# A two-layer hybrid trunk on one core: TensorE in the order of the source, with the mixers' steps placed by a running estimate of each engine's time

## The chip, the cores and the metric

The kernel runs on one core of a Trainium2 chip. The metric is the device time of one execution in microseconds (us), taken as the median of several runs. The profile of one execution gives the time of every instruction on TensorE (PE), VectorE (DVE), ScalarE (ACT), GpSimd (POOL) and of the DMA issues on SyncE (SP).

## The reference

One inference step of a decoder trunk with two layers, for a prompt of 256 tokens and 8 x 4 sample tokens with the same weights, so 288 columns. All is float32, and the width is 1024.

```python
def mixer_block(x, ...):                      # x += mixer_block(x)
    h = rmsnorm(x, p['norm_mix_g'])
    (q_a, k_a, v_a, x_b, y_b, q_c, k_c, v_c, r_c, a_c, g_a, g_b, g_c) = jnp.split(h @ p['w_in'], offs, axis=-1)
    ...   # o_a: sliding-window attention (swa), 8 heads, 2 K/V heads, window 128, sinks
    xc, new_lru_buf = causal_dwconv(x_b, lru_buf, p['lru_conv_w'], p['lru_conv_b'])
    hr, new_h = rg_lru(xc, lru_h, ...)        # gates, then h[t] = a[t] h[t-1] + b[t]   (the scan)
    o_b = jax.nn.gelu(y_b) * hr
    log_alpha = jax.nn.log_sigmoid((a_c @ p['gla_wa2'] + p['gla_ba']).astype(F32)) / GLA_TAU
    o, new_s = gla(q_c * GLA_DK ** -0.5, k_c, v_c, log_alpha, gla_s)     # chunks of 32 tokens
    o_c = rmsnorm(o, p['gla_on_g']) * jax.nn.silu(r_c)
    merged = (jax.nn.sigmoid(g_a) * (o_a @ p['w_branch_a']) + jax.nn.sigmoid(g_b) * (o_b @ p['w_branch_b'])
              + jax.nn.sigmoid(g_c) * (o_c @ p['w_branch_c']))
    return merged @ p['w_out'], ...

x = x + mix
x = x + cross_attn(rmsnorm(x, p['norm_x_g']), mk, mv, p)   # 4 heads over 256 memory tokens
x = x + conv_ffn(rmsnorm(x, p['norm_ffn_g']), ffn_buf, p)  # up, causal conv of 3, SwiGLU, down
```

## The kernel before, in words

**Projections.** A product with a weight matrix goes tile by tile. `weights` (from L149) loads a 128 x 1024 tile by a DMA on SyncE into `wst` (4 buffers, L157), ScalarE rounds it to fp32r (`whi`, 3 buffers, L158), VectorE forms the rest (`wlo`, 3 buffers, L159). `mm3` (L177 to L179) then issues three fp32r matmuls for each 128 rows of the contraction: whi with the high part of the activations, whi with their low part, wlo with the high part. A weight load waits until L159 has read the buffer that it overwrites. The products of two tiles go to one pair in PSUM (`mm`, 2 buffers); small products go to the PSUM pool `sm` (4 buffers).

**Order of a layer.** `mixers` computes Q, K, V of the attention, the low-rank gate input `ac` of gla (L1361, 8 matmuls), then the projections for gla (`qk`, `vf`), lru (`xb`, `gy`), the output gate `sr`, and then gate(0), gate(1), branch(0), branch(1), gate(2), branch(2), with branch 0, 1, 2 for swa, lru, gla; then `wout`, added to the residual X. `cross` and `ffn` follow. Each norm's gain goes into the activations, and its factor `rbc` is multiplied in at the eviction of the products.

**Chains.** The mixers' own small fp32 work is written as generators: `swa` (L462), `lru` (L684), `gla` (L751), norms, memory norms and more. Each step between two `yield`s issues some matmuls and the work of other engines around them. `proj` calls `tick` after every 4 of its 8 contraction blocks (12 matmuls); `tick` (L167) adds to each active chain the credit that the table RATE gives for the current place and runs a step for each whole unit. `Chain.finish` runs what is left.

**Who sets the order.** The text gives an order of instructions; the tile framework then places them on each engine by its own reckoning of readiness and priority (`tc.high_priority`). Only the opening (first norm, Q, K, V of layer 0) is under `manual_schedule`, where the listed engines keep the order of the source. So a step's matmuls can be split up, interleaved with weight matmuls, or moved.

**Lines that the prediction speaks of.** swa: L557 scores (64-row halves), L582 normalizing of the probabilities on VectorE, L586 their transposes, L596 the product with V, L608 the load of its value cache `swav`, L621, L648, L657, L668 the sample part. gla: L755 load of `wa2` (128 KB), L760 its product with `ac`, L816, L846 and L848 scores of a chunk and their masking, L853, L866, L883, L893, L923, L932 states and outputs. lru: L686 `wax`, L688 `lh`, L709 gates, L734 the scan. L242, L219, L253 are the norms, L1092 the load of memory keys, L978 that of the memory itself, L1000 and L1011 its norm.

Of the kernel before, what the change touches and what calls it, by code (L numbers as in the profile page):

```python
# [46 lines left out]
RATE = [  # L47
    dict(swa=1, gla=1),
    dict(swa=4.5, gla=0.5),
    dict(swa=4.5, gla=3.5),  # L50
    dict(swa=5, gla=1),
    dict(swa=4, gla=5),
    dict(swa=5, gla=0.5, lru=3),
    dict(swa=4, gla=4.5, lru=2.5),
    dict(swa=0.5, gla=3, lru=6),
    dict(gla=2.5, lru=2),
    dict(gla=1.5, lru=4),
    dict(gla=5),
    dict(gla=4),
]  # L60

WAIT = 4

PACE = dict(late=(1, 0), mem=(2.5, -2), norm=(3, -1), keys=(2, -0.5), factors=(3.5, -1), flips=(1.5, 1))


# [16 lines left out]
def trunk(ctx: ExitStack, tc: tile.TileContext, a: dict):  # L83
# [7 lines left out]
    gp = ctx.enter_context(tc.tile_pool(name="gp", bufs=8))  # L91
# [70 lines left out]
    pace = dict(rates={}, chains={}, credit={})  # L162

    def pacing(rates, chains, credit):
        pace.update(rates=rates, chains=chains, credit={c: credit for c in rates})

    def tick():  # L167

        for c, n in pace["rates"].items():
            if c in pace["chains"]:  # L170
                pace["credit"][c] = pace["credit"].get(c, 0.0) + n / 4
                while pace["credit"][c] >= 1:
                    pace["credit"][c] -= 1
                    pace["chains"][c].step(1)
# [47 lines left out]
    def norm_prep(l, col):  # L222

        for k in range(KD):
# [4 lines left out]
        for k in range(0, KD, 2):  # L229
# [3 lines left out]
            sqs.append(sq[:, :T])  # L233
        yield
        return (yield from norm_factors(sqs))

    def norm_factors(sqs):
# [12 lines left out]
        yield from wait(2)  # L250
# [42 lines left out]
    def wait(n):  # L293
        for _ in range(n):
            yield

# [28 lines left out]
    class Chain:  # L325
        def __init__(self, gen):
            self.gen, self.out, self.done = gen, None, False

        def step(self, n):
            for _ in range(n):  # L330
                if self.done:
                    return
                try:
                    next(self.gen)
                except StopIteration as e:
                    self.out, self.done = e.value, True

        def finish(self):
            while not self.done:
                self.step(1)  # L340
            return self.out

    def norm_chain(l, col):

        norm = Chain(norm_prep(l, col))
        norm.step(1)
        pacing(dict(n=PACE["norm"][0]), dict(n=norm), PACE["norm"][1])
        return norm

    def opening():  # L350
# [70 lines left out]
        norm = Chain(norm_factors(sqs))  # L421
        pacing(dict(n=4), dict(n=norm), -1)

        def rest(i, out):
            for k in range(KD):
                c = slice(k * P, (k + 1) * P)
                mm3(out[:, :T], hi[i][:, c], lo[i][:, c], xh[:, k, :], xl[:, k, :], k == 0, k == KD - 1)
                if k % 4 == 3:
                    tick()
# [32 lines left out]
    def swa(l, Q, KV):  # L462
# [140 lines left out]


# [79 lines left out]
    def lru(l, xb, gy):  # L684
# [66 lines left out]
    def gla(l, got):  # L751
# [191 lines left out]


# [9 lines left out]
        yield from wait(WAIT)  # L954
# [18 lines left out]
    def mem_load(l, mh, ml):  # L973
# [5 lines left out]
        yield  # L979
# [126 lines left out]
    def cross(l, mem, mh, ml, kcs, vcs):  # L1106
        norm = norm_chain(l, C_GX)
        pace["rates"]["m"], pace["chains"]["m"] = PACE["late"][0], mem
        pace["credit"]["m"] = PACE["late"][1]
        km = mem_k(l, mem, mh, ml)  # L1110
        rbc = norm.finish()
        knorm = Chain(mem_k_norm(l, km))
        knorm.step(1)
        pacing(dict(n=PACE["keys"][0]), dict(n=knorm), PACE["keys"][1])
        Q, sq, qp = s5t(), s5t(), s5t()
        G.memset(qp, 0.0)
        for h in (0, 2):
# [3 lines left out]
            hs = slice(h, h + 2)  # L1121
            with tc.high_priority(AHEAD):
# [27 lines left out]
        pacing(dict(n=PACE["factors"][0]), dict(n=fac), PACE["factors"][1])  # L1150
# [71 lines left out]
        pacing(dict(n=PACE["flips"][0]), dict(n=flip_s), PACE["flips"][1])  # L1222
# [39 lines left out]
    def ffn(l):  # L1262
# [7 lines left out]
        def up(c):  # L1270
            pm = pmm()
# [377 lines left out]
```

## Time and profile before

| what | us |
|---|---|
| median of 3 runs | 1139.26 (1138.72 to 1141.09) |
| the profiled execution, its own time | 1139.73 |
| its span | 1137.8 |
| TensorE busy | 1121.8 (99%) |
| VectorE busy | 794.6 (70%) |
| ScalarE busy | 617.5 (54%) |
| GpSimd busy | 254.3 (22%) |

The span runs from the first to the last instruction; the execution's own time is 1.9 us longer. Matmuls are pipelined, so that a matmul's length (about 0.30 us for 288 columns) is longer than the distance of two starts; distances of starts tell what TensorE spends. An fp32 matmul has two records. Names of buffers are shown without their numbers: `s` is an activation tile of SBUF, `g` a wide one, `m` a narrow one, `sm` and `mm` PSUM.

### The profile page before, as it was taken

The page shows a single profiled execution, that of the slowest core. Times are in us where ns is not written, and L with a number is a line of the kernel's source. Part 1 is how long each engine was busy: PE and PEld are TensorE (multiplying, and loading weights), DVE is VectorE, ACT ScalarE, POOL GpSimd, SP SyncE. Part 2 cuts the span into 40 slices and gives each one's busy share as a digit, 9 for nine tenths or more (in the row PEclk, how much of TensorE's full clock was granted, in tenths as well). Part 3 has the DMA queues.
Part 4 walks back from the last instruction along what each step waited for, and adds up shares of the span by engine and source line. Part 5 has one row for each costly group of instructions (what it writes and reads, how often), then busy time and mean ns, then how long its engine had stood idle before and what let it go on. Part 6 is the DMA issues. An engine that isn't in the chain of part 4 may idle for free.

```text
span 1137.8 us, 22342 instructions
## 1 busy us (share of the span) xinstructions
PE 1121.8 (99%) x8846; PEld 1063.3 (93%) x8846; DVE 794.6 (70%) x1451; ACT 617.5 (54%) x961; POOL 254.3 (22%) x426
## 2 busy tenths in 40 slices
PE   9999999999999999999999999999999999999998
PEld 8878799999989999999999887999999899999998
DVE  6776586757775887885457775856686678888743
ACT  6545874345555665654445567643464456566532
POOL 0211020201211455550012200202111024555400
PEclk9999999999999999999999999999999999999999
DMA  8844445558466455556545343455585644554662
GB/s 284 274 132 129 131 154 167 157 172 316 154 224 232 149 159 162 163 152 206 173 160 176 119 130 117 139 186 167 187 303 153 202 143 149 167 165 154 185 192 83
DMA packets 62663, 198.11 MB, mean 174 GB/s; under 512 B 7960, under 2 KB 11768, under 8 KB 62560
## 3 DMA queue, kind: packets, MB, share of 16 engines
q1 hardware_dynamic: 59536, 188.55, 51.9%
q0 software_dynamic: 2880, 8.15, 2.0%
q8 instruction: 69, 1.13, 0.4%
q14 instruction: 34, 0.28, 0.1%
q10 hardware_dynamic: 144, 0.00, 0.0%
HBM read 187.35 MB, written 8.95 MB: 173 GB/s over the span
## 4 chain that ended last, share of the span: by engine, by line
PE 90%; DVE 4%; ACT 3%; DMA 2%; issue 1%; POOL 0%; SPq 0%; ACTq 0%; POOLq 0%; DVEq 0%
PE mm L178 25%; PE mm L179 25%; PE mm L177 25%; DVE wlo L159 2%; PE sm L596 1%; ACT whi L158 1%; DMA wst<-in_win 1%; PE sm L557 1%; PE sm L1047 1%; PE sm L932 1%; PE sm L1048 1%; PE sm L1049 1%; PE sm L586 1%; PE sm L1234 1%; PE mm L1173 1%
## 5 line engine op out<-in xcount | busy, mean ns | idle before, releaser
L159 DVE TENSOR_TENSOR wlo<-wst,whi 128x1024 fp32r<-128x1024 f32 (+1 forms) x302 | 374.1, 1240 | 141.8 <-ACT whi L158 140.5
L158 ACT CAST whi<-wst 128x1024 fp32r<-128x1024 f32 (+1 forms) x302 | 312.4, 1036 | 273.0 <-PE mm L178 217.2
L177 PE MATMUL mm<-xh,whi 128*128 128x288 f32 x1536 | 455.7, 297 | 1.4 <-DVE s L1329 1.4
L179 PE MATMUL mm<-xh,wlo 128*128 128x288 f32 x1536 | 456.5, 297 | 0.0
L178 PE MATMUL mm<-xl,whi 128*128 128x288 f32 x1536 | 456.1, 297 | 0.0
L177 PEld LDWEIGHTS mm<-xh,whi 128*128 128x128 f32 x1536 | 289.3, 188 | 8.7 <-issue 5.0
L179 PEld LDWEIGHTS mm<-xh,wlo 128*128 128x128 f32 x1536 | 289.0, 188 | 4.3 <-issue 2.9
L178 PEld LDWEIGHTS mm<-xl,whi 128*128 128x128 f32 x1536 | 289.1, 188 | 3.7 <-DVE xl L227 2.1
L178 PE MATMUL mm<-s,whi 128*128 128x288 f32 (+1 forms) x756 | 222.9, 295 | 1.9 <-DVE s L192 1.9
L177 PE MATMUL mm<-s,whi 128*128 128x288 f32 (+1 forms) x756 | 223.5, 296 | 0.0
L179 PE MATMUL mm<-s,wlo 128*128 128x288 f32 (+1 forms) x756 | 222.1, 294 | 0.0
L178 PEld LDWEIGHTS mm<-s,whi 128*128 128x128 f32 x756 | 142.1, 188 | 2.9 <-DVE s L192 2.8
L177 PEld LDWEIGHTS mm<-s,whi 128*128 128x128 f32 x756 | 142.0, 188 | 2.0 <-issue 1.3
L179 PEld LDWEIGHTS mm<-s,wlo 128*128 128x128 f32 x756 | 142.2, 188 | 0.6 <-DVE wlo L159 0.3
L1296 DVE SCALAR_TENSOR_TENSOR y<-u,prm,y 128x304 f32<-128x304 f32 x176 | 82.5, 524 | 0.0
L1300 POOL TENSOR_TENSOR m<-y 128x256 f32<-128x256 f32 x44 | 60.7, 1380 | 69.1 <-ACT y L1297 66.2
L191 ACT CAST s<-m 128x288 fp32r<-128x288 f32 (+1 forms) x46 | 19.6, 426 | 72.2 <-POOL m L1301 72.2
L1294 ACT ACTIVATE y<-u,prm 128x304 f32<-128x304 f32 x88 | 51.8, 635 | 11.7 <-DVE u L1287 11.7
L1436 POOL TENSOR_TENSOR g<-g,g 128x576 f32<-128x576 f32 x12 | 21.0, 1749 | 160.5 <-DVE g L1434 160.5
L192 DVE TENSOR_TENSOR s<-m,s 128x288 fp32r<-128x288 f32 (+1 forms) x46 | 20.8, 452 | 50.8 <-ACT s L191 50.8
L1283 POOL COPY u<-s 128x32 f32<-128x32 f32 x44 | 46.3, 1053 | 0.6 <-DMA s<-in_fconv 0.6
L232 POOL TENSOR_TENSOR s<-s 128x288 f32<-128x288 f32 x20 | 19.2, 966 | 119.3 <-ACT s L231 119.3
(386 smaller groups left out, 1221.7 us busy)
## 6 DMA issues: line engine op xcount, KB each, us to landing
wst<-in_win SPq DMA_DIRECT2D x98, 512.0 KB, 3.5
wst<-in_up SPq DMA_DIRECT2D x88, 512.0 KB, 3.5
wst<-in_down SPq DMA_DIRECT2D x32, 512.0 KB, 3.7
wst<-in_wbr SPq DMA_DIRECT2D x24, 512.0 KB, 3.5
s<-in_mk SPq DMA_DIRECT2D x16, 512.0 KB, 6.6
wst<-in_wout SPq DMA_DIRECT2D x16, 512.0 KB, 4.2
wst<-in_down SPq DMA_DIRECT2D x16, 384.0 KB, 3.1
g<-in_mv SPq DMA_DIRECT2D x16, 256.0 KB, 4.3
```

The lines of the kernel that those rows point to most:

```text
L158: A.copy(hi[:, :n], st[:, :n])
L159: (E or V).tensor_sub(lo[:, :n], st[:, :n], hi[:, :n].bitcast(F32))
L177: PE.matmul(out, wh, bh, start=first, stop=False)
L178: PE.matmul(out, wh, bl, start=False, stop=False)
L179: PE.matmul(out, wl, bh, start=False, stop=last)
L191: A.copy(hi, src)
L192: V.tensor_sub(lo, src, hi.bitcast(F32))
L1283: G.tensor_copy(us[:, :, :, 0:2], fhist[:, 2 * c : 2 * c + 2])
L1294: A.activation(y[:, i, :WFO], u[:, i, 2:], AF.Identity, scale=w[2], bias=prm[:, l, C_FCB + f : C_FCB + f + 1])
L1296: V.scalar_tensor_tensor(y[:, i, :WFO], u[:, i, j : j + WFO], w[j], y[:, i, :WFO], ALU.mult, ALU.add)
L1300: G.tensor_mul(h[:, :NP_], y[:, 0, :NP_], y[:, 1, :NP_])
L1436: (G if x == 1 or m < KD - 4 else V).tensor_add(acc[m], acc[m], g)
```

## The change

All work of the two layers now runs under `manual_schedule` for TensorE: its instructions keep the order of the source. The other engines are scheduled as before. The tables RATE, WAIT and PACE are gone. Instead a callback, `account`, sees each instruction as it is issued and keeps a running time: `est["pe"]` for TensorE, one for each other engine, and `est["cur"]` for the step being issued. DMA copies are skipped. A chain's next step may run at the first `tick` at which `est["pe"]` has reached the end of its last step's estimated work plus 0.3 us. `tick` is called after every 2 contraction blocks (6 matmuls). `lru` yields until `gla` has finished. The memory chain starts ahead of gate(2) rather than behind branch(2). In layer 1, K and V go to two `sm` tiles before the norm is finished; in `ffn` a third pair of up does; in `cross` the norm is finished after the first pair of wq. The `g` pool has 11 buffers instead of 8.

```diff
-    gp = ctx.enter_context(tc.tile_pool(name="gp", bufs=8))
+    gp = ctx.enter_context(tc.tile_pool(name="gp", bufs=11))
...
+    est = dict(pe=0.0, cur=None, serial=True, busy={})
+    active = {}
+
+    def account(i):
+
+        if not hasattr(i, "engine") or not i.outs or i.opcode == "DMACopy":
+            return
+        e, n = str(i.engine), 1
+        for _, c in i.outs[0].ap[1:]:
+            n *= c
+        if i.opcode == "Matmult":
...
+            est["pe"] = max(est["pe"], est["cur"] or 0.0) + c
+            if est["cur"] is not None:
+                est["cur"] = est["pe"]
+            return
+        c = {"EngineType.DVE": 0.1 + n / 850, "EngineType.Activation": 0.22 + n / 1200}.get(e, 0.15 + n / 600)
+        cur = est["cur"] if est["cur"] is not None and est["serial"] else est["pe"]
+        t = est["busy"][e] = max(est["busy"].get(e, 0.0), cur) + c
+        if est["cur"] is not None:
+            est["cur"] = max(est["cur"], t + 0.1)
+
+    nc.push_inst_callback(account)
 
     def tick():
 
-        for c, n in pace["rates"].items():
...
+        for c in list(active.values()):
+            while not c.done and c.ready <= est["pe"]:
+                c.step()
+
+    class Chain:
...
+        def step(self):
+            est["cur"] = est["pe"]
+            try:
+                more = next(self.gen)
+            except StopIteration as e:
+                self.out, self.done, more = e.value, True, 0.0
+            self.ready = est["cur"] + 0.3 + (more or 0.0)
+            est["cur"] = None
+
+        def finish(self):
+            while not self.done:
+                c = min((c for c in [self, *active.values()] if not c.done), key=lambda c: c.ready)
+                est["pe"] = max(est["pe"], c.ready)
+                c.step()
+            return self.out
...
-            if k % 4 == 3:
+            if k % 2:
                 tick()
...
-    def lru(l, xb, gy):
+    def lru(l, got, xb, gy):
+        while "gla" not in got:
+            yield
...
-        yield from wait(WAIT)
...
-        rbc = norm.finish()
-        knorm = Chain(mem_k_norm(l, km))
...
+            rbc = norm.finish()
             with tc.high_priority(AHEAD):
                 V.tensor_mul(Q[:, hs], pm[:, :, :T], bc(rbc, 2))
...
-        first = [up(0), up(1)]
+        first = [up(0), up(1), up(2, (None, psm(), psm()))]
         rbc = norm.finish()
...
             first = [win(I_Q, 2), win(I_Q + 2, 2)]
+            kv = [psm(), psm()]
+            for j in range(2):
+                proj(kv[j][:, :T], a["win"][l, I_K + j], KD, lambda k: xh[:, k, :], lambda k: xl[:, k, :])
             rbc = norm.finish()
...
-        gate(0, 7)
-        gate(1, 8)
-        branch(0, 9)
-        branch(1, 10)
-        gate(2, 11)
-        branch(2, 11)
+        gate(0)
+        gate(1)
+        branch(0)
+        branch(1)
         mh = [s5v(4, NP_, F32R), s5v(4, NP_, F32R)]
         ml = [s5v(4, NP_, F32R), s5v(4, NP_, F32R)]
-        mem = Chain(mem_load(l, mh, ml))
-        mem.step(1)
-        pacing(dict(n=PACE["mem"][0]), dict(n=mem), PACE["mem"][1])
+        mem = active["mem"] = Chain(mem_load(l, mh, ml))
+        gate(2)
+        branch(2)
...
-    for l in range(L):
-        cross(l, *mixers(l))
-        ffn(l)
+    with tc.manual_schedule(engines={mybir.EngineType.PE}):
+        for l in range(L):
+            cross(l, *mixers(l))
+            ffn(l)
+    nc.remove_inst_callback(account)
...
-    nc = bacc.Bacc("TRN2", target_bir_lowering=False, num_devices=1)
+    nc = bacc.Bacc("TRN2", target_bir_lowering=False, num_devices=1, dynamic_dma_scratch_size=8192)
```

The following pieces show the order on an engine; the lines of the changed kernel have numbers of their own (L204 to L206 are L177 to L179 of before, L474 and L475 are L466 and L467, L771 is L760, L857 is L846, L859 is L848, L590 is L582). `sm_461<-m_413,m_457` reads: written to sm, from m 413 and m 457.

TensorE, layer 0, around the first step of gla (m_503 before and m_457 after are wa2, m_411 and m_413 are ac). Before, 74 weight matmuls after L1361:

```order
L179 MATMUL mm_514<-xh,wlo_517 128x288
L177 MATMUL mm_514<-xh,whi_587 128x288
L178 MATMUL mm_514<-xl,whi_587 128x288
L760 MATMUL sm_507<-m_411,m_503 128x288
L760 MATMUL sm_510<-m_411,m_503 128x288
L493 MATMUL sm_533<-s_495,cst 32x256 x4
L494 MATMUL sm_534<-m_496,cst 32x288
```

After, six weight matmuls after the same 8 matmuls:

```order
L204 MATMUL mm_416<-xh,whi_418 128x288
L205 MATMUL mm_416<-xl,whi_418 128x288
L206 MATMUL mm_416<-xh,wlo_419 128x288
L474 MATMUL sm_429<-cst,s_91 128x128 x2
L475 MATMUL sm_429<-cst,s_91 32x128
L771 MATMUL sm_461<-m_413,m_457 128x288
L771 MATMUL sm_464<-m_413,m_457 128x288
```

The product with wa2 has moved ahead by 68 weight matmuls.

SyncE, layer 0, the loads around wa2 (in_wa). Before:

```order
L686 DMA s_1193<-in_wax 128x1024
L157 DMA wst_745<-in_win 128x1024
L688 DMA lh_1195<-in_lh 128x32
L608 DMA s_1248<-in_swav 128x1024
L157 DMA wst_793<-in_win 128x1024
L755 DMA m_503<-in_wa 128x256
L1092 DMA s_2957<-in_mk 128x1024
```

After:

```order
L697 DMA s_1717<-in_wax 128x1024
L137 DMA wst_706<-in_win 128x1024
L699 DMA lh_1719<-in_lh 128x32
L617 DMA s_1813<-in_swav 128x1024
L1103 DMA s_3008<-in_mk 128x1024
L766 DMA m_457<-in_wa 128x256
L1103 DMA s_3010<-in_mk 128x1024
```

The weight load that stood directly ahead of wa2 has moved behind, and a load of memory keys stands in its place; the weight load two places further up (wst_745, wst_706) stands ahead of wa2 in both.

TensorE in layer 0, a chunk's scores of gla, with s_838 and s_839, s_724 and s_725 the scaled q and k; each of the two PSUM tiles belongs to one half of the rows. Before:

```order
L179 MATMUL mm_981<-xh,wlo_1046 128x288
L846 MATMUL sm_970<-s_838,s_839 128x128 x2
L177 MATMUL mm_981<-xh,whi_1045 128x288
L846 MATMUL sm_971<-s_838,s_839 128x128 x2
L853 MATMUL sm_1008<-cst,s_839 128x128 x2
```

After:

```order
L857 MATMUL sm_1061<-s_724,s_725 128x128
L857 MATMUL sm_1062<-s_724,s_725 128x128
L857 MATMUL sm_1061<-s_724,s_725 128x128
L857 MATMUL sm_1062<-s_724,s_725 128x128
L204 MATMUL mm_1043<-xh,whi_1045 128x288
```

The four matmuls stand together and change the half each time; before, two of one half, a weight matmul, and two of the other.

## Rows read from the trace of the kernel before

**Rows 1.** The page: busy us (share) xinstructions; TensorE's granted clock in 40 slices, tenths.

```profile
PE 1121.8 (99%) x8846; PEld 1063.3 (93%) x8846; DVE 794.6 (70%) x1451; ACT 617.5 (54%) x961; POOL 254.3 (22%) x426
PEclk9999999999999999999999999999999999999999
```

**Rows 2.** Windows: stretch us, each engine's busy us (instructions), clock, DMA share, GB/s.

```profile
950.00:1000.00 50.00, 50.00 (x381) 50.00 (x380) 41.30 (x80) 31.60 (x48) 26.91 (x48) 1.00 0.49 159
```

**Rows 3.** Waits of TensorE: line <- engine, tile, line waited for: us, times, longest.

```profile
PE mm L177 <- DVE s L1329: 1.4, 2, 0.7
PE sm L536 <- DVE g L520: 1.2, 2, 0.9
PE mm L418 <- ACT xh L373: 1.2, 1, 1.2
PE sm L586 <- DVE s L582: 0.9, 1, 0.9
PE sm L760 <- DMA m<-in_wa: 0.5, 1, 0.5
```

**Rows 4.** Timeline of TensorE, L846: start, length us, line, operation, shape, xrecords.

```profile
81.60 0.71 PE L846 MATMUL sm<-s,s 64*128 64x128 f32 x4
82.24 0.40 PE L177 MATMUL mm<-xh,whi 128*128 128x288 f32 x1
...
647.58 0.71 PE L846 MATMUL sm<-s,s 64*128 64x128 f32 x8
648.22 0.44 PE L853 MATMUL sm<-cst,s 128*128 128x128 f32 x2
```

**Rows 5.** Timeline of TensorE, L557 with 256 columns.

```profile
640.31 1.13 PE L557 MATMUL sm<-s,s 64*128 64x256 f32 x8
...
641.96 1.13 PE L557 MATMUL sm<-s,s 64*128 64x256 f32 x4
```

**Rows 6.** Timeline of TensorE, L596 in layer 0, each with what follows.

```profile
102.42 1.07 PE L596 MATMUL sm<-s,m 128*64 128x512 f32 x2
103.43 0.44 PE L586 MATMUL sm<-cst,s 128*128 128x128 f32 x2
...
104.48 1.93 PE L596 MATMUL sm<-s,m 128*64 128x512 f32 x6
106.35 0.40 PE L177 MATMUL mm<-xh,whi 128*128 128x288 f32 x1
```

**Rows 7.** Timeline of SyncE's queue, layer 0: start us, us of the issue.

```profile
31.34 0.33 SPq L157 DMA_DIRECT2D wst<-in_win  x1
...
32.19 0.88 SPq L608 DMA_DIRECT2D s<-in_swav  x1
...
37.20 0.43 SPq L755 DMA_DIRECT2D m<-in_wa  x1
```

**Rows 8.** Timeline of TensorE, layer 0: the seventh weight matmul after L1361, and L760.

```profile
30.99 0.29 PE L177 MATMUL mm<-xh,whi 128*128 128x288 f32 x1
...
40.93 1.21 PE L760 MATMUL sm<-m,m 128*128 128x288 f32 x4 [0.46 <-DMA m<-in_wa]
```

**Rows 9.** The line L755, both loads of wa2.

```profile
DMA to landing us min/median/max: 3.4/3.5/3.6
```

**Rows 10.** Timeline of TensorE, layer 1: the seventh weight matmul after L1361.

```profile
596.27 0.29 PE L177 MATMUL mm<-xh,whi 128*128 128x288 f32 x1
```

**Rows 11.** Timeline of SyncE's queue, layer 1: the next weight load (and one more).

```profile
596.58 4.80 SPq L157 DMA_DIRECT2D wst<-in_win  x2
```

**Rows 12.** The line L848 on VectorE: ns min/median/max of 8.

```profile
L848 DVE COPY_PREDICATED g<-cst,sm x8: 431/444/452, 83.8 to 666.8; 128x256 f32<-128x256 int32 x8
```

**Rows 13.** Timeline of VectorE, L582.

```profile
66.77 0.87 DVE L582 TENSOR_SCALAR s<-s,den 128x128 f32<-128x128 f32 x4
```

**Rows 14.** The page's groups: L159, the weight split: busy us, mean ns, idle before.

```profile
L159 DVE TENSOR_TENSOR wlo<-wst,whi 128x1024 fp32r<-128x1024 f32 (+1 forms) x302 | 374.1, 1240 | 141.8 <-ACT whi L158 140.5
```

More of the change, by code (lines that the diff above doesn't have):

```diff
@@ new lines, in trunk, with __init__ @@
+    nc.push_inst_callback(account)
+    def tick():
+        for c in list(active.values()):
+            while not c.done and c.ready <= est["pe"]:
+                c.step()
+    class Chain:
+        def __init__(self, gen):
+            self.gen, self.out, self.done, self.ready = gen, None, False, est["pe"]
+        def step(self):
[12 more added lines that the diff above has]
+            return self.out
@@ L233, in norm_prep @@
             sqs.append(sq[:, :T])
+        est["serial"] = True
         yield
@@ L323, in derived @@
         V.scalar_tensor_tensor(sp8, d_, -8.0, e_, ALU.mult, ALU.add)
[L325 to L341, printed above, removed]
     def norm_chain(l, col):
         norm = Chain(norm_prep(l, col))
-        norm.step(1)
-        pacing(dict(n=PACE["norm"][0]), dict(n=norm), PACE["norm"][1])
+        norm.step()
+        active["norm"] = norm
         return norm
@@ L428, in rest @@
                 if k % 4 == 3:
-                    tick()
+                    quarters[0] += 1
+                    if quarters[0] in (2, 3, 5):
+                        norm.step()
         def prepare(i):
@@ L602, in swa @@
             yield
+        got["swa"] = True
         ks = s5v(NB, 132)
@@ L942, in gla @@
         yield
+        got["gla"] = True
         r = rsqrt(ss, [P, 9], 1.0 / P)
@@ L1341, in mixers @@
                     V.tensor_mul(Q[:, 2 * i : 2 * i + 2], pm[:, :, :T], bc(rbc, 2))
-            plain(I_K, 2, KV[:, 0:2])
+            for j in range(2):
+                with tc.high_priority(AHEAD):
+                    V.tensor_mul(KV[:, j], kv[j][:, :T], rbc)
         else:
@@ L1351, in mixers @@
             derived()
-        chains["swa"] = Chain(swa(l, Q, KV))
+        chains["swa"] = Chain(swa(l, got, Q, KV))
         pm = psm()
@@ L1366, in mixers @@
         qk = s5t()
-        pacing({}, chains, 0)
-        rate(0)
         pm = win(I_QC, 2)
@@ L1399, in mixers @@
         sr = s5t()
-        rate(6)
         for i in (0, 2):
@@ L1406, in mixers, with gate @@
         gates, acc = {}, {}
-        def gate(x, r):
-            rate(r)
+        def gate(x):
             for m in range(0, KD, 2):
@@ L1419, in mixers, with branch @@
         bl = [s5t(F32R), s5t(F32R)]
-        def branch(x, r):
+        def branch(x):
             oh, ol = chains[("swa", "lru", "gla")[x]].finish()
-            rate(r)
             for m in range(0, KD, 2):
```

84 lines of the change are left out of this document (31 added, 53 removed).

## The prediction

> **What bounds the kernel now.** I read the busy shares first, then a quiet stretch, then the waits. TensorE is busy 99% of a span of 1137.8 us, every slice, at a granted clock of 1.00, the higher of its two levels, 2.4 GHz [rows 1]. VectorE (70%) and ScalarE (54%) have room. In a quiet stretch 380 matmuls take 50 us, 0.1315 us each [rows 2]; the 7296 fp32r matmuls of the weights cannot go below 7296 x 0.1315 = 959 us, and the change keeps them all. So only two things can move: what the small matmuls between them cost, and what TensorE waits for. The list of TensorE's waits holds 14 lines, 12 us together; those I use are [rows 3].
>
> The sum is made against the profiled execution's own 1139.73 us, 0.47 above the median; that is taken off at the end.
>
> **Small matmuls.** Each fp32 matmul leaves two records, so x4 is two matmuls. Where two on the same half of the rows follow each other, they take 0.64 us (81.60 to 82.24). Where four alternate halves, all four take the same 0.64 (647.58 to 648.22) [rows 4]. For 256 columns two on the same half and four in alternation are both 1.13 us long [rows 5], 1.06 without the end that the next matmul covers (0.71 against 0.64 above). The order of the source always alternates; the scheduler of before often cut a group into pairs of one half. Counting in the order of before: L846 has 4 groups of four, 3 of them cut, 3 x 0.64 = 1.9 us; L932 has 8 groups of the same shape, 4 cut, 2.6; L557 has 4 groups of 256 columns, two of them cut into same-half pairs (1.06 each) and one cut in two alternating pairs (0.3), 2.4. L596 alone takes 1.01 us, three in alternation 1.87 [rows 6]; after, two and four stand together in each layer. Each further one adds (1.87 - 1.01) / 2 = 0.43, so four cost 2.30 instead of 1.01 + 1.87, twice, and a pair 1.44 instead of 2 x 1.01, once: 1.7. Together 8.6 us. In seven more lines (L893, L866, L242, L883, L586, L219, L923) groups are cut too, and are whole after; pricing each of their matmuls like the one with the same neighbours in before gives up to 6 us, and nothing if what follows a group costs as much as a cut. I take 4.4, so **-13 us**, bounds -8.6 and -14.6.
>
> **Waits that go.** With the steps placed later, those on L520 (1.2), L582 (0.9), L1329 (1.4) and wa2 at L760 (0.5) lose their place in the order: **-4 us** [rows 3], at the least 0. The other waits, those on L192 among them, stand in code that doesn't change.
>
> **A new wait, wa2.** The first step of gla loads wa2 and multiplies by it at once. The planner doesn't count DMAs, so it places the step at the first tick: six weight matmuls after L1361, where before some 70 stood between. On SyncE's queue wa2 stands behind a weight load in both orders, and that load waits for a free buffer, which L159 gives back after L1361. In layer 0 that load goes out at 31.34 and swa's value cache at 32.19, 0.88 us long [rows 7]; in the changed order a memory-key load follows and then wa2, so it goes out at some 33.5. TensorE has done its six matmuls by 30.99 [rows 8], and with three transposes like L853 (x2, 0.44 us [rows 4]) it stands at wa2 by 31.4. When does wa2 land? Alone, 3.4 to 3.6 us after its issue [rows 9], so 36.9 at the earliest. But in before, wa2 went out at 37.20 and landed at 40.8, and TensorE had it at 40.93 after a wait of 0.46 [rows 7, 8]; ahead of it stood a weight tile of 512 KB, and now a memory-key tile of 512 KB. The same bytes have to come in before it, so I take 40.8: a wait of 9.4 us. Bounds: 5.5 (36.9), and 10.1 if the memory keys, whose packets are small, take 0.7 longer. In layer 1 TensorE would be there at 596.27 plus the same 0.4 [rows 10]; the weight load ahead goes out at 596.58 [rows 11], wa2 0.4 later, and lands 3.5 after that [rows 9], at 600.5: 3.8 us. Both: **+13 us**, bounds 9.3 and 13.9.
>
> **New waits of an order that stands still.** Before, the scheduler put a matmul behind what was ready by its own reckoning; now each visit comes where the estimate put it. Example: in both layers L846's four matmuls stand six weight matmuls (0.79 us) ahead of L586. VectorE's order puts L848 twice (0.44 us each [rows 12]) ahead of the four L582 (0.87 for four [rows 13]) that L586 needs. VectorE is through 0.9 + 0.9 = 1.8 us after L846, TensorE after 0.9 plus its own transposes, so some 0.8 us of wait, twice. At the second L586 pair, and at L958, L648 and L269, VectorE's order also has a weight split or an eviction ahead; 0.4 us each, in both layers, gives 3.2. Some of it hides behind the later visits: **+4 us**, bounds 0 and 12 (the rival below).
>
> **Edits costed at nothing.** Memory loads beside gate(2): the first use is 300 matmuls (39 us) later and that stretch has DMA to spare; were its cover gone, two 512 KB loads. K and V, and the third pair of up, in the small PSUM tiles before norm.finish: no line of the waits names the norm's factor there by more than 0.2 us, so there is nothing to gain. Scan mixer last: its last VectorE work stands some 100 matmuls (13 us) ahead of the branch that needs it. More g buffers and less scratch: nobody waits for either. The opening has the same order.
>
> **Sum.** 1139.7 - 13 - 4 + 13 + 4 = 1139.7 on the scale of the profiled run, **1139.3** on that of the median; I put it at 1139. The bounds of the terms, taken halfway in each direction, give 1136 to 1142 for this case. A difference under 0.2% (2.3 us) can't be told from none.
>
> **Rival 1, faster: transfers overtake.** If wa2 isn't held up by the tile ahead, it lands at 36.9, and the wait is 5.5 instead of 9.4 (-3.9). If also the seven lines give their 6 us (-1.6) and the standing order costs 2 rather than 4 (-2): 1131.8. For it: a landing of 3.4 to 3.6 in both layers, busy queue or not [rows 9].
>
> **Rival 2, slower: TensorE's clock falls behind the wait.** The longest single waits of before are 1.2 us [rows 3], and the clock is 1.00 throughout [rows 1], so no row shows what 9.4 us of idling do. At 1.2 GHz each matmul takes 0.13 us more. If the low level outlasts the wait by as long as the wait was, 36 matmuls run in 9.4 us rather than 71, and 4.7 us are lost; for a shorter time I take 3: 1142.3, and 1144 if the wait of layer 1 does it too. The Trainium skill (TensorE: Matmul & The Clock Gate, in the section Part 1: The HAM clock gate) says just that: idleness takes the array to half rate, and only sustained work brings it back. No run here shows it yet.
>
> **Rival 3, slower: VectorE's order decides.** From the point where the VectorE work ahead of what a visit needs is longer than the six weight matmuls between two visits (0.79 us), every such visit waits; one weight split there (1.24 us [rows 14]) is enough. There are 107 visits; if 24 wait 0.5 us each, that is 12 instead of 4: 1147.3. Against it: the estimate knows VectorE's queue, and counts a weight split at 0.1 + 1024 / 850 = 1.30 us, no less than it takes.
>
> **Rival 4, slower: the groups were cut because their operands weren't there.** Then the order doesn't do what it says: TensorE waits for the whole group where before it did half of it early, and half of the 13 comes back: 1145.8. Against it: none of the cut lines but L586 and L866 stands in the waits.
>
> **How the numbers follow.** The forecast's case 0.40 (0.10 of it faster, 0.23 within, 0.07 slower), rival 1 0.26 (faster), rival 2 0.18 (0.06 within, 0.12 slower), rival 3 0.11 and rival 4 0.05 (slower). So faster by over 0.2% 0.36, within 0.2% 0.29, slower 0.35. Cases of both signs hold most of the chance, so the likeliest one's own range (1136 to 1142) stands beside the whole: 1128, rival 1 with wa2's lower bound in full, to 1148, rival 3 with a little of rival 2.
>
> **What would show it.** Right: in the profile after, TensorE waits for the DMA of wa2 twice, near 31 us for 9 and near 590 us for 4; L846, L932 and L557 stand in groups of x8, with VectorE's L582 a new name of 1 to 2 us in the waits. Rival 1: the first of those waits under 6.5 us. Rival 2: a slice of 35 to 45 us with a clock under 0.9. Rival 3: waits on VectorE of over 8 us more. Wrong altogether: no wait on wa2, or groups still cut.

## The result

The changed kernel takes 1158.36 us (median of 4 runs, 1156.28 to 1160.03), the kernel before on the same chip 1139.62: a ratio of 1.0162, 95% interval 1.0138 to 1.0186. It is 18.7 us slower, where 1139 was forecast and the range ended at 1148. The profiled execution took 1156.28 us with a span of 1154.5, 16.7 more than the 1137.8 of before. One run further down, of f_wa2mem, had a mean clock of 0.59 and took 1802 us; it is left out.

The page of the changed kernel, with busy times, TensorE's busy share and its granted clock in 40 slices, answers [rows 1]:

```profile
PE 1115.5 (97%) x8846; PEld 1060.2 (92%) x8846; DVE 797.6 (69%) x1454; ACT 630.0 (55%) x971; POOL 258.4 (22%) x426
PE   9699999999999999999998999999999999999998
PEclk9899999999999999999999998999999999999999
```

VectorE and GpSimd have about the work of before. ScalarE is busy 12.5 us more: its trace holds 40 loads of an activation table (ACT_TABLE_LOAD, 1.28 us each) where before's holds 30; the estimate doesn't count them, and what they cost was not tried by itself. TensorE is busy 6 us less in a span that is 17 us longer. One slice, around 29 to 58 us, stands at 6 tenths with a lower clock, and the clock is lower in the slice around 693 to 722 us as well. Its waits by what was waited for (times, longest), to be held against [rows 3]:

```profile
PE sm L771 <- DVE m L509: 9.5, 1, 9.5
PE sm L594 <- DVE s L590: 6.4, 4, 2.3
PE sm L771 <- DVE s L509: 4.1, 1, 4.1
PE mm L204 <- DVE g L1440: 3.8, 4, 1.5
PE sm L1022 <- DVE rm L1018: 1.6, 1, 1.6
```

L771 is the product with wa2, L594 are the transposes behind L590. That VectorE's L509 is named at L771 is the releaser that came last by the records; the load itself shows who it was (and in the trace of e_mem the same two waits stand under the load's name). SyncE's queue and the product in layer 0, answering [rows 7, 8], the same in layer 1, and the landing times of the two loads, answering [rows 9]:

```profile
30.80 0.33 SPq L137 DMA_DIRECT2D wst<-in_win  x1
31.64 0.43 SPq L617 DMA_DIRECT2D s<-in_swav  x1
32.12 0.43 SPq L1103 DMA_DIRECT2D s<-in_mk  x1
33.24 0.33 SPq L766 DMA_DIRECT2D m<-in_wa  x1
```

```profile
40.48 2.26 PE L771 MATMUL sm<-m,m 128*128 128x288 f32 x4 [9.54 <-DVE m L509]
```

```profile
605.98 0.33 SPq L137 DMA_DIRECT2D wst<-in_win  x1
606.36 0.42 SPq L766 DMA_DIRECT2D m<-in_wa  x1
```

```profile
609.97 0.72 PE L771 MATMUL sm<-m,m 128*128 128x288 f32 x2 [4.13 <-DVE s L509]
```

```profile
DMA to landing us min/median/max: 3.5/5.3/7.1
```

33.24 + 7.1 = 40.3: the load lands and the product starts at once. In layer 1 it lands 3.5 us after its issue, at 609.8, and the wait there is 4.1. Both times it lands right behind the 512 KB tile issued ahead of it: the memory keys issued at 32.12 landed 7.9 us later, at 40.0, and the weight tile of 605.98 at 609.4.

What that idling does to TensorE's clock is new. Windows of the changed kernel; behind the engines' busy times stand granted clock, DMA share and GB/s:

```profile
36.00:40.00 4.00, 0.00 (x0) 0.00 (x0) 3.75 (x13) 0.00 (x0) 0.53 (x1) 0.50 1.05 414
42.00:44.00 2.00, 2.00 (x9) 1.80 (x8) 1.00 (x2) 1.50 (x3) 0.00 (x0) 0.50 0.31 121
44.00:46.00 2.00, 2.00 (x18) 1.18 (x17) 0.00 (x0) 1.95 (x2) 0.00 (x0) 0.97 0.00 0
...
708.00:710.00 2.00, 2.00 (x15) 1.77 (x12) 0.73 (x3) 0.00 (x0) 0.00 (x0) 0.50 0.54 215
```

The clock falls to 0.50 (1.2 GHz of 2.4) within the wait and stays there for 3.6 us of work behind it: 9 matmuls in 2 us, then 18. It falls again behind the wait of layer 1, and at 706 behind a wait of 2.3 us at L594.

To add this up I took the distances between the starts of all matmuls from the first to the last: what lies between the end of one and the start of the next is a wait; half of the busy time at a clock of 0.50 is the clock's loss; the rest is what the matmuls take at full clock. All of the experiments below stand in the same table (us, each from its one profiled run).

| kernel | matmuls at full clock | waits | lost to the clock | sum |
|---|---|---|---|---|
| before | 1119.9 | 11.1 | 1.7 | 1132.7 |
| changed | 1108.4 | 34.2 | 6.9 | 1149.5 |
| e_wa2 | 1108.0 | 25.0 | 6.8 | 1139.8 |
| e_fill (its 94 matmuls of filling, 12.4, left out; with them the sum is 1145.3) | 1109.0 | 22.2 | 1.7 | 1132.9 |
| e_mem | 1108.1 | 34.0 | 8.1 | 1150.3 |
| e_probs | 1106.7 | 39.6 | 15.2 | 1161.5 |
| e_lru | 1108.4 | 45.7 | 14.3 | 1168.4 |
| e_paired | 1108.8 | 29.3 | 3.1 | 1141.2 |
| e_wa2pair | 1109.4 | 19.3 | 3.4 | 1132.0 |
| e_manual | 1103.2 | 39.3 | 11.5 | 1154.0 |
| e_sched | 1112.5 | 11.5 | 0.0 | 1124.0 |
| f_wa2 | 1112.4 | 12.8 | 0.0 | 1125.2 |
| f_wa2mem | 1112.4 | 10.8 | 3.4 | 1126.6 |
| f_lru | 1118.6 | 8.2 | 0.0 | 1126.8 |

So the change brings 11.5 us by cheaper matmuls and pays 23.1 of waits and 5.2 of clock: 16.8.

### The profile page after: what moved, and what is told of

Read it like the earlier page. It is cut to its first block, busy times and chain, and to the rows that moved or that the text cites. A ratio compares the mean times of both kernels' runs of the same rounds, so it can differ in the third digit from the quotient of the medians.

```text
span 1154.5 us, 22367 instructions
## 1 busy us (share of the span) xinstructions
PE 1115.5 (97%) x8846; PEld 1060.2 (92%) x8846; DVE 797.6 (69%) x1454; ACT 630.0 (55%) x971; POOL 258.4 (22%) x426
## 5 line engine op out<-in xcount | busy, mean ns | idle before, releaser
L204 PE MATMUL mm<-xh,whi 128*128 128x288 f32 x1488 | 449.2, 302 | 1.5 <-DVE g L1440 1.5
L206 PE MATMUL mm<-xh,wlo 128*128 128x288 f32 x1488 | 443.6, 298 | 0.3 <-DVE wlo L139 0.2
L205 PE MATMUL mm<-xl,whi 128*128 128x288 f32 x1488 | 441.4, 297 | 1.0 <-DVE xl L255 1.0
L204 PEld LDWEIGHTS mm<-xh,whi 128*128 128x128 f32 x1488 | 281.9, 189 | 14.2 <-issue 11.3
L206 PEld LDWEIGHTS mm<-xh,wlo 128*128 128x128 f32 x1488 | 281.5, 189 | 5.0 <-DVE wlo L139 1.3
L205 PEld LDWEIGHTS mm<-xl,whi 128*128 128x128 f32 x1488 | 281.7, 189 | 2.8 <-DVE xl L255 1.9
L204 PE MATMUL mm<-s,whi 128*128 128x288 f32 (+1 forms) x756 | 223.7, 296 | 2.3 <-DVE g L1440 2.3
L206 PE MATMUL mm<-s,wlo 128*128 128x288 f32 (+1 forms) x756 | 222.5, 294 | 0.0
L204 PEld LDWEIGHTS mm<-s,whi 128*128 128x128 f32 x756 | 142.3, 188 | 4.5 <-issue 2.3
L206 PEld LDWEIGHTS mm<-s,wlo 128*128 128x128 f32 x756 | 142.2, 188 | 0.5
L218 ACT CAST s<-m 128x288 fp32r<-128x288 f32 (+1 forms) x46 | 19.6, 427 | 78.9 <-POOL m L1315 78.9
L260 POOL TENSOR_TENSOR s<-s 128x288 f32<-128x288 f32 x20 | 17.6, 879 | 140.0 <-ACT s L259 132.9
L1442 POOL TENSOR_TENSOR g<-g,g 128x576 f32<-128x576 f32 x12 | 25.1, 2092 | 84.4 <-DVE g L1440 60.4
L1294 POOL COPY u<-s 128x32 f32<-128x32 f32 x44 | 41.3, 940 | 0.0
```

The costliest lines, as they stand in the source:

```text
L204: PE.matmul(out, wh, bh, start=first, stop=False)
L205: PE.matmul(out, wh, bl, start=False, stop=False)
L206: PE.matmul(out, wl, bh, start=False, stop=last)
L218: A.copy(hi, src)
L1294: G.tensor_copy(us[:, :, :, 0:2], fhist[:, 2 * c : 2 * c + 2])
L1442: (G if x == 1 or m < KD - 4 else V).tensor_add(acc[m], acc[m], g)
```

## The experiments

The theory to be tested: three things cost the time, the load of wa2, VectorE's order ahead of swa's transposes, and the clock behind both; a whole group of small matmuls is the gain. The rivals were that VectorE and not the load holds wa2 up, that the clock costs nothing, that parts other than the standing order (memory chain, scan last) are to blame, and that the steps' places cost the time, whoever orders them.

**e_wa2: the load earlier.**

```diff
             nc.sync.dma_start(wac, a["wac"][l])
+            wa2 = got["wa2"] = m1(2 * P)
+            nc.sync.dma_start(wa2, a["wa2"][l])
```

(and `wa2 = got["wa2"]` in gla in place of its own load)

> The changed kernel with one edit: wa2 is loaded right behind wac in both layers, instead of in gla's first step. Main theory (TensorE's two waits at the product with wa2 are for the load, and TensorE's clock falls behind each): both waits, 9.5 and 4.1 us, go, and with them the stretches at half clock behind them, which cost 1.8 and 1.7 us: 1158.4 - 13.6 - 3.5 = 1141.3 us, and the granted clock is 1.00 from 30 to 45 us. Rival (VectorE's rotary work L509, which the profile names as the releaser, is what TensorE waits for): the waits stay at over 8 us, time above 1155. Rival (another late operand takes the wait over): half comes back as a wait within 10 us of the same place, about 1150.

Measured: 1145.86 us (1144.92 to 1146.64), 12.5 less than the changed kernel, 1.0045 of the kernel before (1.0029 to 1.0061). Its waits:

```profile
PE sm L594 <- DVE s L590: 6.5, 4, 2.3
PE sm L246 <- ACT m L504: 2.6, 2, 2.1
PE sm L769 <- DVE m L1379: 0.8, 2, 0.5
```

The wait on L509 is gone with the load, so it was the load. 13.7 us of wait went, and 4.5 came back, most of it in two places: the transposes L246 a little later now wait for a ScalarE copy (2.6), and the product itself for `ac` (0.8). So the third of the expected outcomes came in part: another late operand took over a third of the wait. The expected 3.5 of clock didn't come: the clock fell at 40.35, behind that wait of 2.1, and at 132.5, behind L594 in layer 0, where it hadn't in the changed kernel.

**e_fill: the wait kept, TensorE kept busy in it.**

```diff
         zc, za = s5t(), s5t()
+        fill, keep = psm(), dict(est)
+        for _ in range(68 if l == 0 else 26):
+            PE.matmul(fill[:, :T], xh[:, 0, :P], xl[:, 0, :], start=True, stop=True)
+        est.update(pe=keep["pe"], cur=keep["cur"])
```

> The changed kernel with useless work in the two waits for wa2: 68 matmuls of 288 columns in layer 0 and 26 in layer 1, into a PSUM tile that nobody reads, ahead of the product with wa2 (8.9 and 3.4 us at full clock, less than the waits). wa2 comes no earlier, so the wait as such is still paid. Theory that the clock falls because TensorE is idle: the clock stays at 1.00 from 30 to 45 us and from 605 to 615 us, and the time falls by 1.8 + 1.7 = 3.5 us, to 1154.9. Rival (the slow stretch costs nothing, since other engines set the pace there): 1158.4 within 1.2. Rival (the load is held up by something TensorE does): the time rises by the added work, to over 1165.

Measured: 1153.09 us (1152.09 to 1153.47), 5.3 less than the changed kernel, with 94 useless matmuls more. A timeline and a window (in this kernel L771 is the filling and L775 the product with wa2):

```profile
31.46 9.19 PE L771 MATMUL sm<-xl,xh 128*128 128x288 f32 x68
40.79 0.48 PE L775 MATMUL sm<-m,m 128*128 128x288 f32 x1
```

```profile
38.00:42.00 4.00, 3.87 (x27) 3.46 (x26) 3.92 (x9) 0.45 (x1) 0.54 (x1) 1.00 1.04 409
```

The product starts where it did, at 40.8 instead of 40.5, and the clock is 1.00. At wa2 idling was what made it fall, and the fall has a price of its own: the table's 6.9 goes to 1.7. That is 1.7 more than the two places are worth, because the slow stretch at L594 is shorter here (3.4 us instead of 6.8). The clock's share differs between runs of one kernel too: the four of the changed kernel have mean clocks of 0.986 to 0.991.

**e_mem: the memory chain behind branch(2) again.**

```diff
-        mem = active["mem"] = Chain(mem_load(l, mh, ml))
         gate(2)
         branch(2)
+        mem = active["mem"] = Chain(mem_load(l, mh, ml))
```

> The changed kernel with one part undone: the chain that loads and splits the memory starts behind branch(2) again, as before the change, not ahead of gate(2). Theory (the memory splits L996 stand ahead of the evictions L1440 on VectorE, and their norm's wait at L1022 grew from 0.6 to 1.6 us): TensorE's waits on L1440 (3.8 us in all) and 1 us at L1022 go: 1158.4 - 4.5 = 1153.9. Rival (they move: the same VectorE work now delays the residual or the memory norm): 1158.4 within 1.2, with new waits of 3 to 5 us between 235 and 265 us. Rival (the place of the memory chain is worth something, as the change means it): slower, over 1161.

Measured: 1157.70 us (1154.18 to 1161.38): no difference that these runs can tell. Its waits:

```profile
PE sm L1022 <- DVE ry L239: 2.4, 1, 2.4
PE mm L204 <- DVE g L1440: 2.2, 3, 1.5
```

In layer 0 the wait of 1.5 on the eviction L1440 is gone, and the memory norm's own wait grew from 1.6 to 2.4; the L1440 of layer 1 stays, so the memory chain had no part in that one. The rival that the waits only move was right, with 0.9 us at the memory norm, at 304 us, where 3 to 5 between 235 and 265 were expected.

**e_probs: priority for the normalizing of the probabilities.**

```diff
-            V.tensor_add(den, den, es)
-            V.reciprocal(den, den)
+            with tc.high_priority(2 * AHEAD):
+                V.tensor_add(den, den, es)
+                V.reciprocal(den, den)
...
+            with tc.high_priority(2 * AHEAD):
+                for h in range(8):
+                    V.tensor_scalar(pp[h // 4][:, h % 4, :nk], pp[h // 4][:, h % 4, :nk], den[:, h : h + 1], None, ALU.mult)
+            yield
             for kv in range(2):
-                for j in range(4):
-                    h = kv * 4 + j
-                    V.tensor_scalar(pp[kv][:, j, :nk], pp[kv][:, j, :nk], den[:, h : h + 1], None, ALU.mult)
                 for kb in range(blk + 1):
```

> The changed kernel with two edits in swa: the normalizing of the probabilities (reciprocal and all eight L590) has priority on VectorE over evictions and weight splits, and one more yield stands between it and the transposes L594. Theory (VectorE's order, with an eviction and a weight split ahead of L590, makes TensorE wait): the four waits on L590, 6.4 us, go, and so does the half clock from 706 to 713 us behind one of them, 3.4 us: 1158.4 - 9.8 = 1148.6. Without the clock 1152. Rival (the work put behind is needed just as soon): waits of the same size on the weight split or the eviction, 1155 to 1159.

Measured: 1168.11 us (1166.87 to 1169.67), 9.8 more instead of less. Its waits:

```profile
PE mm L204 <- ACT s L218: 6.7, 2, 3.3
PE sm L936 <- DMA g<-in_glas: 4.0, 2, 2.1
```

The waits on L590 are gone, as meant. But the order of the later steps is another one: gla's sample states now come up before their loads, and lru's output (L218) is 3.3 us late at the first matmul of branch(1), in each layer. The clock falls in more places than in the changed kernel: 15.2 us. I put the new waits down to the yield, which moves every later step; what the priority alone does was not tried, so this stays an argument.

**e_sched: TensorE placed by the framework again.**

```diff
-    with tc.manual_schedule(engines={mybir.EngineType.PE}):
-        for l in range(L):
+    for l in range(L):
```

> The changed kernel with one part undone: TensorE is placed by the framework again (no manual_schedule over the two layers); the estimate, the ticks and the other parts stay. Theory (the order that stands still brings 11.7 us by whole groups of small matmuls and costs 23 us of waits and some 6 of half clock): groups are cut again, the waits for wa2 and L590 go: 1158.4 + 11.7 - 21 - 6 = 1143 us, TensorE's waits under 16 us in all. Rival (the places of the steps, not the standing order, cost the time): waits stay over 25 us, time over 1155.

Measured: 1133.08 us (1131.68 to 1134.18), 25.3 less than the changed kernel and 0.9941 of the kernel before (0.9917 to 0.9964). The largest wait:

```profile
PE mm L204 <- DVE g L1440: 3.9, 5, 1.5
```

Waits and clock are what the theory said (11.5 and 0), and the rival, that the steps' places cost the time whoever orders them, is out. It missed where the cheaper matmuls come from: of the 11.5 us that the change gains in them, 7.4 stay without the standing order. Line by line, the groups L857, L565, L604, L877 and L904 cost the same as in the changed kernel, to 0.1 us; the sample states L943 cost 7.6 us against 5.1, and L934 0.7 more. So the framework left most groups as they were. That the estimate's places are the reason is not shown: the other parts of the change are in this kernel too.

**e_paired: halves of the rows one after the other.** The loops are swapped in three places, as here:

```diff
-            for hp in range(2):
-                for hh in range(2):
+            for hh in range(2):
+                for hp in range(2):
                     rows = slice(hh * 64, hh * 64 + 64)
                     PE.matmul(pa[hh][:, hp * P : hp * P + P], kk[rows, hp, ts], qt[rows, hp, ts], start=True, stop=True)
```

> The changed kernel with the loops around three groups of small matmuls swapped, so that matmuls of one half of the rows follow each other: the scores of gla's chunks (L857, 4 groups of 4), its sample states (L943, 8 groups of 4) and the scores of swa (L565, 4 groups of 4 with 256 columns and 2 of 8 with 128). Nothing is moved between engines. Theory (alternating halves is what a whole group is worth): 4 x 0.64 + 8 x 0.64 + 4 x 1.06 + 2 x 1.6 = 15.1 us more, 1173, a little less where a wait behind a group shrinks. Rival (the order within a group is worth nothing, only its standing together): 1158.4 within 1.5.

Measured: 1148.58 us (1147.99 to 1150.36): 9.8 less where 15 more was expected. Two things are in it. First, a group of four on L857, with what follows, in the changed kernel and in this one:

```profile
92.83 0.71 PE L857 MATMUL sm<-s,s 64*128 64x128 f32 x8
93.47 0.40 PE L204 MATMUL mm<-xh,whi 128*128 128x288 f32 x1
```

```profile
92.75 0.72 PE L857 MATMUL sm<-s,s 64*128 64x128 f32 x8
93.40 0.40 PE L204 MATMUL mm<-xh,whi 128*128 128x288 f32 x1
```

0.64 and 0.65 us: the order within the group is worth nothing here (the scores of swa lose 1.1 us in all by it, the sample states gain 0.5). The two halves of the rows run side by side in either order; what costs is a pair with nothing of the other half beside it, as at 81.60 in [rows 4]. The Trainium skill (TensorEngine Tiling (Array Packing), in Key Properties under Tiling Modes) says that tiles work independently and can run matmuls in parallel, and these rows agree: four in 0.65 us, two in 0.64.

Second, the time fell because VectorE's order came out otherwise. VectorE and TensorE at L594 in layer 0, changed kernel:

```profile
133.16 0.65 DVE L590 TENSOR_SCALAR s<-s,den 128x256 f32<-128x256 f32 x2
133.73 1.11 DVE L947 SCALAR_TENSOR_TENSOR g<-g,elast,sm 128x128 f32<-128x128 f32 x4
134.77 0.74 DVE L1421 TENSOR_TENSOR g<-mm,rbc 128x576 f32<-128x576 f32 x1
135.48 1.23 DVE L139 TENSOR_TENSOR wlo<-wst,whi 128x1024 fp32r<-128x1024 f32 x1
136.62 1.66 DVE L590 TENSOR_SCALAR s<-s,den 128x256 f32<-128x256 f32 x6
```

```profile
134.34 0.38 PE L594 MATMUL sm<-cst,s 128*128 128x128 f32 x2
137.02 0.59 PE L594 MATMUL sm<-cst,s 128*128 128x128 f32 x2 [2.31 <-DVE s L590]
```

and TensorE in e_paired, where all of L590 was done before the evictions:

```profile
134.36 0.60 PE L594 MATMUL sm<-cst,s 128*128 128x128 f32 x4
134.89 0.65 PE L934 MATMUL sm<-g,s 128*32 128x128 f32 x16
```

In the changed kernel TensorE has two of four transposes and waits 2.3 us for the rest, which stand behind four updates, an eviction and a weight split. In e_paired it doesn't wait, and with the two waits the fall of the clock at 706 is gone: 4.9 of waits and 3.8 of clock by the table. That the loop order moved VectorE's instructions is an accident of the framework; as an experiment it gives the price of that wait.

**e_wa2pair: both edits, standing order kept.**

> The changed kernel, standing order kept, with the edits of e_wa2 and e_paired. e_paired was faster than the changed kernel by 9.8 us because VectorE's order came out with L590 ahead of the eviction and the weight split, so that the two waits of 2.3 us and the half clock behind them were gone. Theory (these waits, wa2's and the clock behind both are what made the changed kernel slower): the two gains add up, 1158.4 - 12.5 - 9.8 = 1136, and the kernel is no slower than the one before. Rival (they share a cause or open the next wait): 1141 or more.

Measured: 1137.06 us (1134.55 to 1139.46), 0.9972 of the kernel before (0.9959 to 0.9984). The gains add up within 1.1 us. Without these waits the standing order is 0.3% faster than the kernel before.

**e_lru: lru doesn't wait for gla.**

```diff
-        while "gla" not in got:
-            yield
```

> The changed kernel with one part undone: lru doesn't wait for gla to finish. Theory (with the scan last, the split of lru's output stands ahead of the evictions L1440 of branch(1) and delays them: 1.5 us in layer 1, 0.4 twice at the first matmul of the branch): 1158.4 - 2.5 = 1156. Rival (lru's steps among gla's put more work ahead of what a visit needs): slower, over 1161. Rival (no difference): 1157 to 1160.

Measured: 1175.93 us (1175.14 to 1178.74), 17.6 more. Its waits:

```profile
PE sm L594 <- DVE s L590: 13.4, 6, 4.3
```

VectorE ahead of the longest of them:

```profile
141.10 0.17 DVE L584 TENSOR_TENSOR den<-den,es 128x8 f32<-128x8 f32 x1 [2.71 <-ACT s L581]
141.30 0.20 DVE L585 RECIPROCAL den<-den 128x8 f32<-128x8 f32 x1
141.54 0.88 DVE L590 TENSOR_SCALAR s<-s,den 128x256 f32<-128x256 f32 x3
142.33 1.45 DVE L730 SCALAR_TENSOR_TENSOR s<-s,s 128x1248 f32<-128x1248 f32 x1
```

The wait on L1440 is gone, as the theory said, but that was the small side; the rival was right. VectorE itself waits 2.7 us for swa's exponentials (L581) on ScalarE, which here also has lru's work, and L594 waits 4.3 us; then a long step of lru (L730) stands among the L590, and L594 waits another 1.2. Of the parts undone one at a time, "scan mixer last" is worth most to the standing order.

**f_lru: the same in the framework's order.**

> e_sched with lru not waiting for gla. In the order that stands still this cost 17.5 us (e_lru). Theory (that was waits: work of lru on VectorE and ScalarE came ahead of what the next visit needed, and TensorE couldn't do anything else): the framework moves the visits, so less than 4 us of the 17.5 remain: 1133 to 1137. Rival (it is too much work in one place, whoever orders it): over 1142.

Measured: 1134.01 us (1133.58 to 1135.22), 0.9 more than e_sched (1131.68 to 1134.18), which is not to be told from none. Of the 17.6 nothing stays: the framework cuts the groups (1118.6 in the table instead of 1112.5; L565, L604 and L857 cost 5.6 us more) and has fewer waits (8.2).

**e_manual: the standing order alone, on the kernel before.** The loop over the layers of the kernel before is put under `manual_schedule` for TensorE, and nothing else is changed.

> The kernel before with one part of the change alone: TensorE in the order of the source over both layers; the steps stay where the tables RATE, WAIT and PACE put them. Theory (whole groups bring 11.7 us in any order that keeps them; waits come from where the steps stand): groups whole, so -11.7; wa2's product comes 48 weight matmuls after L1361 instead of 6, so a wait of 3.5 us in layer 0 and none in layer 1; waits on VectorE and others of 5 to 15 us, as the tables were made for an order that moves: 1136 to 1148. Rival (a standing order waits wherever it stands): 1155 or more.

Measured: 1161.63 us (1160.86 to 1162.92), 1.0191 of the kernel before (1.0171 to 1.021). Its waits:

```profile
PE sm L586 <- DVE s L582: 14.8, 4, 4.9
PE sm L760 <- DMA m<-in_wa: 4.5, 1, 4.5
PE sm L760 <- DVE s L501: 2.7, 1, 2.7
```

The groups are whole (1103.2), but it waits 39.3 us, 28 more than the kernel before, where I had expected 8 to 18 more, and it loses 11.5 to the clock. The wait at wa2 in layer 0 was 4.5 (3.5 expected), and 2.7 came in layer 1 where I had none. The rival, that a standing order waits wherever it stands, was right. With this run the standing order is priced twice: 22 us on the steps of the kernel before (1161.6 against 1139.7), 25 us on those of the changed kernel (1158.4 against 1133.1).

**f_wa2 and f_wa2mem: towards a better kernel.** e_sched with the load of e_wa2, and that with the memory chain as in e_mem.

> The changed kernel with TensorE placed by the framework (as in e_sched) and wa2 loaded behind wac (as in e_wa2). Theory (in e_sched 1.6 us of TensorE's waits are still for wa2, and nothing else hangs on it): 1133.1 - 1.6 = 1131.5 us, no wait on wa2. Rival (another operand of the same step takes over, as the sums of squares L504 did in e_wa2 with 2.1 us): 1133.1 within 1.

> f_wa2 with the memory chain behind branch(2) again. Theory from e_mem (its place gives and takes the same: waits on the evictions L1440 of 1.5 us go, the memory norm's wait at L1022 grows by 1 to 2): the time of f_wa2 within 1.5 us. Rival (with TensorE placed by the framework the memory norm's wait is filled with other matmuls): 1.5 to 2.5 us less than f_wa2.

Measured: 1132.49 us (1131.08 to 1133.8) and, for f_wa2mem, 1131.68 (1129.89 to 1134.13, five runs). f_wa2 is 0.9927 of the kernel before (0.9911 to 0.9944), f_wa2mem 0.9924 (0.9906 to 0.9942). Neither is to be told from e_sched, nor from the other: the rival of f_wa2 was right, a ScalarE copy takes the wait over. One line of f_wa2's waits:

```profile
PE sm L246 <- ACT m L504: 1.8, 1, 1.8
```

e_sched, one line away from the changed kernel, is the version to keep: 0.6% faster than the kernel before, 2.2% faster than the changed one.

## Why the prediction was wrong

**The wait for wa2 was right**, to the place and the size: 9.5 and 4.1 us where 9.4 and 3.8 were forecast, by the step that the same bytes have to come in first: landed at 40.3, 40.8 forecast. Rival 1 (a transfer that overtakes) is out: in both layers it lands 0.3 to 0.4 us behind the 512 KB tile ahead of it. What differs is what was still under way: in layer 0 the DMA share was 1.05 between 36 and 40 us, and it took 7.1 us; in layer 1 it was 0.65 between 606 and 608 us, and it took 3.5.

**The small matmuls were nearly right in size, in part by luck, and half wrong in the reason**: 11.5 us instead of 13. Line by line (each distance put down to the earlier of the two matmuls, without waits and half clock) L846, L932 and L557 gave the 1.9, 2.6 and 2.4 forecast, L596 3.7 instead of 1.7, the seven other lines 7.7 instead of 4.4: 18 us. Against it the weight matmuls take 6.2 us more, which the forecast left at nothing. In e_manual, whose steps stand where the tables put them, they don't, so it goes with the new places of the steps; why is open. And what counts is that the two halves stand together; e_paired shows that alternating them adds nothing. The count of cut groups, from which the size came, is the same by either reason. Rival 4 (whole groups that have to wait) is seen at L594 alone; L857, L943, L565 and L604 are not in the list of waits.

**The waits that go** went in part: L520's and L1329's are no more in the list. L582's 0.9 didn't go but grew to the 6.4 at L594, and wa2's is the new wait; below, the whole 4 us are counted as gone and these two as new.

**The new waits of the standing order are the step that failed**: +4 was taken with a bound of 12, and they are 13.4: of 34.2 us of waits 13.7 are wa2's, which leaves 20.5 where 11.1 - 4.0 = 7.1 were left of before. Of the 9.4 too little, 3.8 stand at one place. For the second L586 pair I took 0.4 us, with "a weight split or an eviction ahead"; there stood four updates, an eviction and a weight split, and it was 2.3, in both layers. I had read that order, and priced it as one operation. Another 3.8 are the waits on the evictions L1440, which had no term. L846 ahead of L586 came out as said, 0.9 for 0.8, and L958 and L269 with 0.4 each. The sentence against rival 3, that the estimate knows VectorE's queue, was the wrong argument: the estimate runs VectorE in the order of the source, and the framework doesn't. Evictions and weight splits have priority in the kernel's text, stand behind the step in the source, and ran ahead of it: some 1.9 of the 2.3 us. By its own sign, waits on VectorE of over 8 us more, rival 3 came true: without wa2's they rose from 7.8 to 19.0 us in all. In e_lru and e_manual the waits on the same line take up to 4.3 and 4.9 us.

**Rival 2 came true as well**, with 5.2 us where 3 were given it. I had written that the clock is 1.00 throughout in the kernel before. That row has 40 slices of 28 us and shows 9 for 0.9 and more. A finer window of the kernel before would have shown it, as would TensorE's timeline:

```profile
694.00:696.00 2.00, 1.53 (x7) 1.53 (x8) 2.00 (x6) 1.97 (x3) 0.00 (x0) 0.71 0.15 59
696.00:698.00 2.00, 2.00 (x6) 1.50 (x6) 1.28 (x6) 1.97 (x3) 0.68 (x1) 0.50 0.00 0
```

```profile
694.47 0.40 PE L177 MATMUL mm<-xh,whi 128*128 128x288 f32 x1 [0.69 <-DVE s L1329]
...
695.07 0.44 PE L177 MATMUL mm<-xh,whi 128*128 128x288 f32 x1
695.30 0.44 PE L178 MATMUL mm<-xl,whi 128*128 128x288 f32 x1
```

There, behind some 6 us of small matmuls with waits of 0.2 to 0.7 us among them, the clock was at half, and each weight matmul started some 0.24 us after the last instead of 0.13. So the price could have been read, and the condition was milder than a wait of 9 us. The Trainium skill (TensorE: Matmul & The Clock Gate, in the section Part 1: The HAM clock gate) was right that idleness takes the array to half rate, and e_fill bears it out: the same wait, filled, 1.00.

**The rivals were treated as excluding each other.** The range ended at rival 3 with a little of rival 2. (The forecast's own range was added up wrongly too: its bounds, halfway in each direction, give some 1135 to 1148, not 1136 to 1142. And of the 7296 weight matmuls 384 have 256 columns, so the 959 us are some 6 too many; no term rests on that.) In this kernel the clock fell behind waits of the standing order, so the two come together: 13.4 - 4 = 9.4 from the one and 5.2 from the other make 14.6 on top of the forecast, and on the scale of the profiled run 1139.7 + 14.6 + 1.5 (of the small matmuls) + 0.7 (of wa2) = 1156.5, against 1156.3 measured.

**Edits costed at nothing**: the memory chain's place gives and takes the same (e_mem). The scan's place was not without a price: the split of lru's output, 1.36 us in one piece, stands ahead of L1440 in layer 1 and costs 1.5 us. The margin of 13 us was none in layer 0 (the split ends at 212.7, where branch(1) waits 0.2 us for it) and some 4 us in layer 1, because ScalarE and GpSimd stand in that chain too: the split waits 1.8 us for ScalarE's L218, which had waited for GpSimd's L754. Undoing it costs ten times that. The remaining edits (K and V, the third pair of up, the norm in `cross`, the buffers) were not undone one by one.

Still open: how much of a step's lateness the priorities alone cause. e_probs changed the priority and the steps' places at once, and in e_paired VectorE's order changed by accident.

## What to carry to other kernels

An order that stands still is only as good as the plan behind it: the plan must know the loads and the order in which the other engines will really run, else every late operand is a wait on the engine that sets the time. The changed kernel's plan, with its other parts, was worth more in the hands of a scheduler that may still move things (e_sched, 0.994) than as a fixed order (1.016); what the plan alone gives was not separated from the other parts. And when a change adds waits to a busy TensorE, price the clock behind each wait with it; the windows of a few us show it, the row of 40 slices doesn't.

## What the runs showed of the hardware that I had not expected

The clock doesn't fall behind every wait of one length. The same wait of 2.3 us at L594 left it at 1.00 in layer 0 of the changed kernel (137 us) and took it to 0.50 in layer 1 (706 us); in e_wa2 it was the other way round, with a fall at 132.5 and none at 700. In e_sched, with no wait over 1.5 us, it doesn't fall before the end.

Matmuls on the two halves of the rows run side by side even when both of one half are issued first: four in 0.65 us, while one pair alone takes 0.64.
